# Stores of the gated scan output moved to GpSimd's queue, a third buffer for the chunk decays, and the group norm's roots turned on TensorE before they are written out

## The chip, the cores and the metric

One core of a Trainium2 chip runs the program. The core has TensorE (PE in the profile, with PEld for its weight loads), VectorE (DVE), ScalarE (ACT), GpSimd (POOL) and SyncE (SP), and 16 DMA engines that carry every transfer, whichever engine issued it. The metric is the device time of one execution in microseconds.

## The reference, cut to what matters

One sequence of 1024 rows of 1024 channels goes through a block of two mixers and an FFN, all in float32:

```
h  = rmsnorm(x);  u = h @ w_in              # split into z, xbc, dt, s_b, s_c, s_x, g_a, g_b
xbc = silu(causal_conv4(xbc) + b);  xs, B, C = split(xbc)
dt = softplus(dt_raw + dt_bias);  a = -exp(a_log)
y  = chunked_scan(xs, dt, a, B, C) + d_skip * xs       # 4 groups of 8 heads, head size 64, state 128
y  = y * silu(z)
y  = y * rsqrt(mean(y*y over the 512 channels of a group) + eps) * ssd_norm_w
branch_a = y @ w_ssd_proj
branch_b = (s_b * causal_conv3(s_c * s_x)) @ w_sconv_proj
x  = x + (sigmoid(g_a) * branch_a + sigmoid(g_b) * branch_b) @ w_o
x  = x + swiglu(rmsnorm(x));  out = rmsnorm(x)
```

The change touches the line with `rsqrt` (its root per row and group), the stores of the `y` that it makes, and the buffers of `exp(cumulated dt*a)` in the scan.

## The kernel before, in words

Every instruction is put on its engine in the order in which the Python code issues it; no scheduler moves anything. Semaphores are added where a tile, a buffer or a DRAM tensor is used again. An engine, and each engine's DMA queue, works strictly in that order: a DMA that waits holds up every later DMA of the same queue. A DMA issued from SP or ACT also waits until the eighth one before it, counted over both queues, has landed.

The large products are done with Strassen-Winograd forms (seven products of half-size blocks, named by `n` 1 to 7; T1 to T4 and S1 to S4 are sums of blocks). Every float32 operand is split into a high part (`hi`, by ACT) and a low part (`lo`, by DVE), and each product takes three matmuls (lines 81 to 83 and 673 to 675). SBUF is one pool of 47 pages of 4 KB a partition (`page`), given out in turn; what takes a page waits for the last user of it. PSUM is 8 banks (`bank`).

The program's stages on the profile's clock: the input product in half-size forms (up to about 620 us), the last 20 tiles of it computed directly (`direct_tile`, about 620 to 960 us), the products of the two mixers (`gv` and `gy`, tiles gb and gd), then `w_o`, and the FFN from about 1260 us on.

The scan runs inside the direct stage. `scans` is a generator; `direct_tile` advances it one step at a time between its matmuls, alternating `part1(j)` and `part2(j-1)` for the 32 pairs of group and 128-row chunk. `part1` reads the chunk (tiles bc, x1) and makes the masked decay matrix ab; `part2` makes poff (old state by C, multiplied by the decays eb), the new state st, and pdg. `part2(j)` ends with `prep_eb(j + 2)`: two DMAs of SP that fill an eb tile (line 387). The tag eb has two buffers, so that this DMA waits until DVE's line 476 of the same `part2(j)` has read the other use of the buffer.

After every fourth chunk `norm` starts, another generator that goes one piece forward in each scan step: it loads silu(z) (two DMAs of SP, line 507), multiplies (line 513), squares, sums over partitions with ones on TensorE (pq, line 527), makes the root (`rstd_of`, DVE and ACT, tiles gv and gr), writes the 128x4 roots to DRAM as 4 rows of 128 (line 530, GpSimd's queue) and reads them back broadcast over the partitions (rbc, line 532). Five steps later it scales y (line 537) and stores it to y_g from SP's queue (line 541). For the second half of a group it also makes T1 to T4 and stores them to yt_d (line 552). There are 8 norms: 8 root stores, 12 stores of y_g and 16 of yt_d. The last two norms end during the first product of the mixers, `gv`, where SP also loads its chunks (tiles ca and cb, from lines 728, 735 and 1098), four chunks ahead of TensorE; their high and low parts are made two chunks ahead.

Of the kernel before, what the change touches and what calls it, by code (L numbers as in the profile page):

```python
# [8 lines left out]
F32 = mybir.dt.float32  # L9
F32R = mybir.dt.float32r  # L10
AF = mybir.ActivationFunctionType
ALU = mybir.AluOpType

P = 128
S = 1024
D = 1024
KT = D // P
# [3 lines left out]
H = G * HPG  # L21
# [18 lines left out]
def hybrid_block(ctx: ExitStack, tc: tile.TileContext, x, nmw, w_in, cw, cb, dtb, alog, dsk, snw,  # L40
                 wssd, scw, wsc, wo, nfw, wg, wu, wd, fnw, out):
    nc = tc.nc
# [5 lines left out]
    cp = ctx.enter_context(tc.tile_pool(name="cp", bufs=1))  # L48
    pp = ctx.enter_context(tc.tile_pool(name="pp", bufs=NPAGES))
    sp = ctx.enter_context(tc.tile_pool(name="sp", bufs=2))  # L50
# [5 lines left out]
    def nm(s):  # L56
        cnt[0] += 1
        return f"{s}_{cnt[0]}"

    def page(s, shape=(P, 1024), dt=F32):  # L60
        return pp.tile(list(shape), dt, tag="pg", name=nm(s))

    def bank(s):
        return sm.tile([P, 512], F32, tag="sm", name=nm(s))
# [21 lines left out]
    ident = cp.tile([P, P], F32, name="ident")  # L86
# [9 lines left out]
    def rstd_of(ssq, n, s):  # L96
        shp = list(ssq.shape)
        v = sp.tile(shp, F32, tag="rv", name=nm(s + "v"))
        nc.vector.tensor_scalar(v, ssq, 1.0 / n, EPS, op0=ALU.mult, op1=ALU.add)
        r = sp.tile(shp, F32, tag="rr", name=nm(s + "r"))  # L100
        nc.scalar.activation(r, v, AF.Sqrt)
        nc.vector.reciprocal(r, r)
        q = sp.tile(shp, F32, tag="rq", name=nm(s + "q"))
        nc.vector.tensor_mul(q, r, r)
        nc.vector.tensor_mul(q, q, v)
        nc.vector.tensor_scalar(q, q, -0.5, 1.5, op0=ALU.mult, op1=ALU.add)
        nc.vector.tensor_mul(r, r, q)
        return r
# [20 lines left out]
    def rows_scale(src, xn, ssq, act=(), parts=1):  # L129
        r = rstd_of(ssq, D, "n")  # L130
        for c in range(parts):
            cs = slice(c * D // parts, (c + 1) * D // parts)
            for i in range(len(src)):
                if i in act:
                    nc.scalar.activation(xn[i][:, cs], src[i][:, cs], AF.Copy, scale=r[:, i:i + 1])
                else:
                    nc.vector.tensor_scalar_mul(xn[i][:, cs], src[i][:, cs], r[:, i:i + 1])
        return xn
# [85 lines left out]


    xt = [page("x") for _ in range(NT)]
    wdt_s = sp.tile([P, KT * H], F32, tag="eb", name="wdts").rearrange("p (k h) -> p k h", h=H)
    warm = cp.tile([P, 1], F32, name="warm")
    nc.scalar.activation(warm, epst, AF.Sqrt)
    for i in range(4):  # L230
        nc.sync.dma_start(xt[i], x[i * P:(i + 1) * P, :])


    ra = cp.tile([96, P], F32, name="ra")
    nc.gpsimd.dma_start(ra, cw[0].rearrange("k (i p) -> (k i) p", p=P))
    rb = cp.tile([80, P], F32, name="rb")
    nc.gpsimd.dma_start(rb[0:8, :], nmw.rearrange("o (i p) -> (o i) p", p=P))
    nc.gpsimd.dma_start(rb[8:16, :], nfw.rearrange("o (i p) -> (o i) p", p=P))
    nc.gpsimd.dma_start(rb[16:40, :], cb.rearrange("o (i p) -> (o i) p", p=P))
# [11 lines left out]
    def small_loads():  # L251
        nc.gpsimd.dma_start(d2, dsk.rearrange("o (i j) -> (o i) j", j=2))
        nc.gpsimd.dma_start(dtbc, dtb.rearrange("o h -> h o"))
        for q in range(4):
            nc.gpsimd.dma_start(al[32 * q:32 * q + 32, :], alog.rearrange("o h -> h o"))
    rd = cp.tile([16, 2, 64], F32, name="rd")
    cols = cp.tile([P, 192], F32, name="cols")
    cwc = lambda k, i: cols[:, k * 24 + i:k * 24 + i + 1]
    nmc = cols[:, 96:104]
# [14 lines left out]
    y_g = [dr.tile([512, S], F32, name=f"y_g{i}") for i in range(G)]  # L274
# [98 lines left out]
    bufs, cur = {}, {}  # L373
# [8 lines left out]
    def prep_eb(j):  # L382
        g, c = items[j]
        if c > 0:
            eb = bufs["e", j] = sp.tile([P, 4, P], F32, tag="eb", name=nm("eb"))
            for i in range(2):
                nc.sync.dma_start(eb[64 * i:64 * i + 64, :, :],
                                  e_d[c, g * HPG:g * HPG + HPG].rearrange("(r j) l -> j r l", j=2)[i].partition_broadcast(64))
# [70 lines left out]
    def part2(j):  # L459
# [37 lines left out]
        if c % 4 == 3:  # L497
            norms.append(norm(g, c // 4, *cur.pop(j // 4)["y"]))
        if j + 2 < len(items):
            prep_eb(j + 2)  # L500

    def norm(g, hf, y0, y1):

        ys, o = (y0, y1), slice(hf * 512, hf * 512 + 512)
        for i in range(2):
            z = page("z", HB)
            nc.sync.dma_start(z, z_g[g][256 * i:256 * i + 256, o].rearrange("(r p) l -> p r l", p=P))
            if i == 0:
                zs = z
        yield  # L510
        yield
        for y, z in zip(ys, (zs, z)):
            V.tensor_mul(y, y, z)
        yield
        yield
        sa, sb = page("sa", HB), page("sa", HB)
        nc.scalar.activation(sa, y0, AF.Square)
        nc.scalar.activation(sb, y1, AF.Square)
        yield
        V.tensor_add(sa, sa, sb)  # L520
        V.tensor_add(sa[:, 0], sa[:, 0], sa[:, 1])
        yield
        yield
        yield
        pq = bank("pq")
        for c in range(4):
            nc.tensor.matmul(pq[:, c:c + 1], sa[:, 0, c * P:(c + 1) * P], ones, start=True, stop=True)
        rs = rstd_of(pq[:, 0:4], INNER // G, "g")
        rd_ = rs_d[2 * g + hf]
        nc.gpsimd.dma_start(rd_.rearrange("c l -> l c"), rs)  # L530
        rbc = page("rbc", (P, 512))
        nc.gpsimd.dma_start(rbc, rd_.rearrange("c l -> (c l)").partition_broadcast(P))
        for _ in range(5):
            yield
        for r in range(4):
            z = ys[r // 2][:, r % 2]
            V.scalar_tensor_tensor(z, z, snc(4 * g + r), rbc, op0=ALU.mult, op1=ALU.mult)
            if r % 2:
                yield
                if hf == 0 or r > 1:  # L540
                    nc.sync.dma_start(y_g[g][128 * (r - 1):128 * (r + 1), o].rearrange("(r p) l -> p r l", p=P),
                                      ys[r // 2])
        if hf == 0:
            kept[g] = ys
            return

        b11, b21 = kept.pop(g)
        b12, b22 = ys
        t1, t2 = page("s1", HB), page("s2", HB)
        for t, a, b, f in ((t1, b11, b12, "T1"), (t2, t1, b22, "T2"), (b12, b12, b22, "T3"), (b21, b21, t2, "T4")):  # L550
            V.tensor_add(t, a, b)
            nc.sync.dma_start(yt_d[f][256 * g:256 * g + 256, :].rearrange("(k p) f -> p k f", p=P), t)
            yield

    def scans():


        def step_norms():
            for n in list(norms):
                if next(n, 0) == 0:  # L560
                    norms.remove(n)

        def one(f, j):
            f(j)
            step_norms()

        want(0, 0)
        want(0, 2)
        prep(0)
        prep(1)  # L570
        prep_eb(1)
        yield
        prep2(0)
        for j in range(len(items)):
            one(part1, j)
            yield
            if j > 0:
                one(part2, j - 1)
                yield
        one(part2, len(items) - 1)  # L580
        yield
        while norms:
            step_norms()
            yield
# [118 lines left out]
    def weight_forms(s, kind, kh):  # L703
        return {f"{kind}{i}": dr.tile([kh * P, 576], F32, name=f"{s}_d{i}")[:, 0:512] for i in range(1, 5)}
# [4 lines left out]
    vt_d, yt_d = weight_forms("vt", "T", 4), weight_forms("yt", "T", 8)  # L709
# [816 lines left out]
    nc.tensor.transpose(pc[:, 0:96], ra, ident[:96, :96])  # L1526
    nc.tensor.transpose(pc[:, 96:176], rb, ident[:80, :80])
    nc.scalar.activation(cols[:, 0:176], pc[:, 0:176], AF.Copy)
    r0 = rows_scale(*a0, act=(3,), parts=2)
    raw0, raw1 = ([], []), ([], [])  # L1530
    turned = {}
# [190 lines left out]
```

## Time and profile before

| | |
|---|---|
| median of 3 runs | 1922.33 us (1921.34 to 1922.79) |
| profiled execution | 1926.88 us, its span 1925.1 us, so 1.8 us lie around the span |
| TensorE busy | 1885.6 us, 98% of the span |
| DVE, ACT, GpSimd busy | 68%, 50%, 8% |
| granted clock of TensorE | 0.995 of full speed in the mean |
| DMA | 411.97 MB, 214 GB/s in the mean |
| DMA issues of SP's and ACT's queues | 323.27 and 29.36 MB; GpSimd's queue 57.79 MB |

TensorE is busy nearly all the time, so a change can gain only in the 39.5 us in which it is not, and in stretches in which its clock is granted at the lower of its two levels (1.2 in place of 2.4 GHz). The profiled execution is 0.24% longer than the median of the runs.

### The profile page before, as it was taken

The numbers are of one execution on the slowest core, as the hardware profiler recorded it, in microseconds if no ns is written. First come the engines' busy times: TensorE is split into PE (matmuls) and PEld (weight loads), VectorE is DVE, ScalarE is ACT, GpSimd is POOL, SyncE is SP. The second block draws the span as 40 slices with busy tenths as digits, with TensorE's granted clock in tenths as the row PEclk, the third lists the DMA queues.
The fourth block names the chain that finished last, engine by engine and source line by source line (L and its number), as shares of the span: only waits on it lengthen the run. The fifth ranks groups of instructions, "written<-read, shape, count | busy, mean of one in ns | idle before, by whom it ended". The sixth has DMA issues, their size and how long they took to land.

```text
span 1925.1 us, 24069 instructions
## 1 busy us (share of the span) xinstructions
PE 1885.6 (98%) x8897; PEld 1548.5 (80%) x8897; DVE 1299.5 (68%) x1688; ACT 969.8 (50%) x1533; POOL 151.0 (8%) x168
## 2 busy tenths in 40 slices
PE   7999999999999999999989999999999999999998
PEld 5688888888888888887768888887888888888886
DVE  7667878777775778897867648877444444456465
ACT  5545454445445987877655454464333333345333
POOL 1010111010100000000000000101221121100000
PEclk9999999999999999999989999999999999999999
DMA  5197999978959567888799866836998788867552
GB/s 179 58 258 176 241 230 236 230 203 224 276 137 292 184 210 212 263 239 227 210 265 328 292 220 211 202 122 141 222 207 210 195 193 200 218 259 286 195 194 111
DMA packets 344774, 411.97 MB, mean 214 GB/s; under 512 B 17416, under 2 KB 223936, under 8 KB 344656
## 3 DMA queue, kind: packets, MB, share of 16 engines
q1 hardware_dynamic: 292016, 323.27, 52.9%
q0 software_dynamic: 44576, 57.79, 18.8%
q10 hardware_dynamic: 8064, 29.36, 4.0%
q8 instruction: 70, 1.15, 0.2%
q14 instruction: 48, 0.39, 0.1%
HBM read 320.56 MB, written 143.15 MB: 241 GB/s over the span
## 4 chain that ended last, share of the span: by engine, by line
PE 84%; DMA 6%; DVE 5%; ACT 4%; issue 1%; SPq 0%; ACTq 0%; DVEq 0%
PE pb L673 5%; PE pb L674 5%; PE pb L675 5%; PE gb L673 5%; PE gb L674 5%; PE gb L675 5%; PE fb L675 4%; PE fb L674 4%; PE fb L673 4%; PE pd L673 4%; PE pd L674 4%; PE pd L675 4%; PE gd L675 3%; PE gd L673 3%; PE gd L674 3%; PE fd L675 3%
## 5 line engine op out<-in xcount | busy, mean ns | idle before, releaser
L77 DVE TENSOR_TENSOR wl<-ws,wh 128x1024 fp32r<-128x1024 f32 x77 | 94.0, 1222 | 121.2 <-ACT wh L76 121.2
L673 PE MATMUL gb<-qh,gh 128*128 128x512 f32 x432 | 168.9, 391 | 1.1 <-DVE h L1126 1.1
L674 PE MATMUL gb<-ql,gh 128*128 128x512 f32 x432 | 168.8, 391 | 0.0
L675 PE MATMUL gb<-qh,gl 128*128 128x512 f32 x432 | 168.8, 391 | 0.0
L675 PE MATMUL fb<-th,wl 128*128 128x512 f32 x352 | 137.0, 389 | 0.8 <-DVE wl L77 0.8
L673 PE MATMUL fb<-th,wh 128*128 128x512 f32 x352 | 137.1, 390 | 0.6 <-ACT wh L76 0.6
L674 PE MATMUL fb<-tl,wh 128*128 128x512 f32 x352 | 136.9, 389 | 0.0
L81 PE MATMUL pr<-th,wh 128*128 128x512 f32 x320 | 131.6, 411 | 0.0
L673 PE MATMUL gd<-qh,gh 128*128 128x512 f32 x324 | 127.2, 392 | 3.8 <-ACT qh L76 3.8
L83 PE MATMUL pr<-th,wl 128*128 128x512 f32 x320 | 125.7, 393 | 4.0 <-DVE wl L984 4.0
L674 PE MATMUL gd<-ql,gh 128*128 128x512 f32 x324 | 127.4, 393 | 0.8 <-DVE ql L77 0.8
L675 PE MATMUL gd<-qh,gl 128*128 128x512 f32 x324 | 127.2, 393 | 0.0
L82 PE MATMUL pr<-tl,wh 128*128 128x512 f32 x320 | 125.1, 391 | 0.0
L76 ACT ACTIVATE qh<-cb 128x1024 fp32r<-128x1024 f32 x98 | 99.9, 1020 | 40.1 <-PE gb L674 17.2
L77 DVE TENSOR_TENSOR ql<-cb,qh 128x1024 fp32r<-128x1024 f32 x98 | 116.0, 1184 | 3.9 <-ACT qh L76 3.7
L675 PE MATMUL fd<-th,wl 128*128 128x512 f32 x264 | 102.7, 389 | 0.0
L673 PE MATMUL fd<-th,wh 128*128 128x512 f32 x264 | 102.7, 389 | 0.0
L674 PE MATMUL fd<-tl,wh 128*128 128x512 f32 x264 | 102.7, 389 | 0.0
L74 DVE SCALAR_TENSOR_TENSOR gl<-ca,gh 128x1024 fp32r<-128x1024 f32 (+1 forms) x60 | 70.6, 1177 | 43.1 <-ACT gh L73 43.0
L673 PEld LDWEIGHTS gb<-qh,gh 128*128 128x128 f32 x432 | 81.5, 189 | 18.2 <-DVE h L1126 1.4
L674 PEld LDWEIGHTS gb<-ql,gh 128*128 128x128 f32 x432 | 81.4, 189 | 17.4 <-DVE ql L77 0.4
L673 PE MATMUL pb<-th,wh 128*128 128x512 f32 x240 | 94.5, 394 | 0.8 <-ACT u L888 0.8
(318 smaller groups left out, 4686.8 us busy)
## 6 DMA issues: line engine op xcount, KB each, us to landing
ws<-in_w_in_dram SPq DMA_DIRECT2D x80, 512.0 KB, 7.2
ws<-in_w_gate_dram SPq DMA_DIRECT2D x77, 256.0 KB, 3.9
ws<-in_w_up_dram SPq DMA_DIRECT2D x77, 256.0 KB, 4.5
ca<-u_d SPq DMA_DIRECT2D x35, 512.0 KB, 5.3
ab<-ac_d SPq DMA_DIRECT2D x32, 512.0 KB, 8.2
xbc_g<-cv ACTq DMA_DIRECT2D x24, 512.0 KB, 6.7
ws<-ws POOLq DMA_DIRECT2D x22, 512.0 KB, 6.4
wd_d<-in_w_down_dram SPq DMA_DIRECT2D x20, 512.0 KB, 9.5
```

The source lines that it names most:

```text
L74: nc.vector.scalar_tensor_tensor(lo, src, -1.0, hi.bitcast(F32), op0=ALU.mult, op1=ALU.subtract)
L76: nc.scalar.activation(hi, src, AF.Copy)
L77: nc.vector.tensor_sub(lo, src, hi.bitcast(F32))
L81: nc.tensor.matmul(o, lh, rh, start=first, stop=False)
L82: nc.tensor.matmul(o, lh, rl, start=False, stop=False)
L83: nc.tensor.matmul(o, ll, rh, start=False, stop=last)
L673: nc.tensor.matmul(o, lh, rh, start=first, stop=False, skip_group_check=True)
L674: nc.tensor.matmul(o, lh, rl, start=False, stop=False, skip_group_check=True)
L675: nc.tensor.matmul(o, ll, rh, start=False, stop=last, skip_group_check=True)
```

## The change: what it does

The 28 stores of y_g and yt_d are issued from GpSimd's queue, not from SP's. The tag eb gets a third buffer. For its room, the constants that are loaded at the start (ra and rb) stand in a page that is given back, and rd in a buffer of the tag st. In `norm`, two steps are put between the root and its store; in the second of them TensorE turns the 128x4 roots to 4x128 (prt), ACT copies them to SBUF (rst), and the store writes 4 whole rows. The wait that follows is four steps in place of five, so that the y of a norm is scaled and stored one step later.

```diff
-    wdt_s = sp.tile([P, KT * H], F32, tag="eb", name="wdts").rearrange("p (k h) -> p k h", h=H)
+    wdt_s = sp.tile([P, KT * H], F32, tag="eb", bufs=3, name="wdts").rearrange("p (k h) -> p k h", h=H)
...
-    ra = cp.tile([96, P], F32, name="ra")
+    consts = page("c")
+    ra, rb = consts[0:96, 0:P], consts[0:80, P:2 * P]
...
-    rd = cp.tile([16, 2, 64], F32, name="rd")
+    rd = sp.tile([P, 512], F32, tag="st", name="rd")[:16, 0:P].rearrange("a (b c) -> a b c", c=64)
...
-            eb = bufs["e", j] = sp.tile([P, 4, P], F32, tag="eb", name=nm("eb"))
+            eb = bufs["e", j] = sp.tile([P, 4, P], F32, tag="eb", bufs=3, name=nm("eb"))
...
         rs = rstd_of(pq[:, 0:4], INNER // G, "g")
+        yield
+        yield
+        prt = bank("prt")
+        nc.tensor.transpose(prt[:4, :P], rs, ident)
+        rst = sp.tile([4, P], F32, tag="rst", name=nm("rst"))
+        nc.scalar.activation(rst, prt[:4, :P], AF.Copy)
         rd_ = rs_d[2 * g + hf]
-        nc.gpsimd.dma_start(rd_.rearrange("c l -> l c"), rs)
+        nc.gpsimd.dma_start(rd_, rst)
         rbc = page("rbc", (P, 512))
         nc.gpsimd.dma_start(rbc, rd_.rearrange("c l -> (c l)").partition_broadcast(P))
-        for _ in range(5):
+        for _ in range(4):
             yield
...
-                    nc.sync.dma_start(y_g[g][128 * (r - 1):128 * (r + 1), o].rearrange("(r p) l -> p r l", p=P),
+                    nc.gpsimd.dma_start(y_g[g][128 * (r - 1):128 * (r + 1), o].rearrange("(r p) l -> p r l", p=P),
                                       ys[r // 2])
...
-            nc.sync.dma_start(yt_d[f][256 * g:256 * g + 256, :].rearrange("(k p) f -> p k f", p=P), t)
+            nc.gpsimd.dma_start(yt_d[f][256 * g:256 * g + 256, :].rearrange("(k p) f -> p k f", p=P), t)
```

On SP's queue, at the end of the direct stage, the loads of the first chunks of `gv` (ca, cb) and the last loads of eb and z stood between stores of y_g and yt_d; this is the order before:

```order
L387 DMA eb_7856<-e_d 64x4x128 x2
L728 DMA ca_7866<-in_w_sconv_proj_dram 128x2x512
L1098 DMA cb_7868<-v_g_128 128x2x512
L387 DMA eb_7964<-e_d 64x4x128 x2
L728 DMA ca_8014<-in_w_sconv_proj_dram 128x2x512
L1098 DMA cb_8016<-v_g_129 128x2x512
L541 DMA y_g_126<-y_6761 128x2x512
L552 DMA yt_d_163<-s_1223_8097 128x2x512
L507 DMA z_8101<-z_g_122 128x2x512
L507 DMA z_8103<-z_g_122 128x2x512
L552 DMA yt_d_164<-s_1224_8098 128x2x512
L728 DMA ca_8154<-in_w_sconv_proj_dram 128x2x512
```

And this is the same place of SP's queue in the changed program:

```order
L387 DMA eb_7872<-e_d 64x4x128 x2
L734 DMA ca_7889<-in_w_sconv_proj_dram 128x2x512
L1104 DMA cb_7891<-v_g_127 128x2x512
L387 DMA eb_7987<-e_d 64x4x128 x2
L734 DMA ca_8035<-in_w_sconv_proj_dram 128x2x512
L1104 DMA cb_8037<-v_g_128 128x2x512
L507 DMA z_8119<-z_g_121 128x2x512
L507 DMA z_8121<-z_g_121 128x2x512
L734 DMA ca_8172<-in_w_sconv_proj_dram 128x2x512
```

Loads alone are left there: the z loads and the third pair of ca and cb have no store ahead of them that waits for DVE.

On GpSimd's queue, in the direct stage, only the root stores (rs_d) and their broadcast loads (rbc) stood, as these rows before show:

```order
L697 DMA vt_d_162<-vt_d_160 256x512
L530 DMA rs_d_132<-gr_5524 128x4x1
L532 DMA rbc_5533<-rs_d_132 128x512
L530 DMA rs_d_133<-gr_5971 128x4x1
L532 DMA rbc_5980<-rs_d_133 128x512
```

In the changed program the same queue holds this, from the second norm on:

```order
L536 DMA rs_d_132<-rst_6092 4x128
L538 DMA rbc_6095<-rs_d_132 128x512
L547 DMA y_g_123<-y_5018 128x2x512
L558 DMA yt_d_162<-s_916_6399 128x2x512
L558 DMA yt_d_163<-s_917_6400 128x2x512
L558 DMA yt_d_164<-y_5017 128x2x512
L536 DMA rs_d_133<-rst_6525 4x128
L538 DMA rbc_6528<-rs_d_133 128x512
L558 DMA yt_d_165<-y_4654 128x2x512
L547 DMA y_g_124<-y_5432 128x2x512
```

The stores of one norm now stand around the root store of the next one; the store of T4 (yt_d_165) stands behind a broadcast load, which waits until its root store has landed.

On DVE, in `gv`, the low parts of the next chunk (gl, ql), the additions that empty the four gd banks (mc) and the scaling of y by rbc come ahead of the last norm's root (gv from pq); this is the order before:

```order
L537 SCALAR_TENSOR_TENSOR y_7198<-y_7198,cols,rbc_8138 128x512 x2
L77 TENSOR_TENSOR gl_8311<-ca_8212,gh_8310 128x1024
L77 TENSOR_TENSOR ql_8315<-cb_8214,qh_8314 128x1024
L1046 TENSOR_TENSOR mc_8248<-mc_8248,gd_8276 128x512
L1046 TENSOR_TENSOR mc_8248<-mc_8248,gd_8277 128x512
L1046 TENSOR_TENSOR mc_8249<-mc_8249,gd_8290 128x512
L1046 TENSOR_TENSOR mc_8249<-mc_8249,gd_8291 128x512
L537 SCALAR_TENSOR_TENSOR y_7199<-y_7199,cols,rbc_8138 128x512 x2
L99 TENSOR_SCALAR gv_8357<-pq_8352 128x4
```

In the changed program DVE has this there:

```order
L77 TENSOR_TENSOR gl_8336<-ca_8237,gh_8335 128x1024
L77 TENSOR_TENSOR ql_8340<-cb_8239,qh_8339 128x1024
L1052 TENSOR_TENSOR mc_8273<-mc_8273,gd_8303 128x512
L1052 TENSOR_TENSOR mc_8273<-mc_8273,gd_8304 128x512
L1052 TENSOR_TENSOR mc_8274<-mc_8274,gd_8317 128x512
L1052 TENSOR_TENSOR mc_8274<-mc_8274,gd_8318 128x512
L543 SCALAR_TENSOR_TENSOR y_7211<-y_7211,cols,rbc_8235 128x512 x2
L543 SCALAR_TENSOR_TENSOR y_7212<-y_7212,cols,rbc_8235 128x512 x2
L99 TENSOR_SCALAR gv_8383<-pq_8378 128x4
```

All four scalings by rbc have come to stand between the emptying of the banks and the last root. On TensorE that root is turned one chunk, 24 matmuls, after its sums; after the other seven sums there are two scan steps, or one chunk and the rest of a tile.

## Rows read from the trace of the kernel before

**Rows 1.** The page's first part: busy time, share of the span, instructions.

```profile
PE 1885.6 (98%) x8897; PEld 1548.5 (80%) x8897; DVE 1299.5 (68%) x1688; ACT 969.8 (50%) x1533; POOL 151.0 (8%) x168
```

**Rows 2.** Waits of PE, 600 to 1100 us: us in total, times, longest.

```profile
PE pr L83 <- DVE wl L984: 4.0, 1, 4.0
PE gd L673 <- ACT qh L76: 3.8, 1, 3.8
PE pq L527 <- DVE mc L1046: 2.6, 1, 2.6
PE poff L475 <- DVE st L484: 1.3, 1, 1.3
PE gd L674 <- DVE ql L77: 0.8, 1, 0.8
```

**Rows 3.** Stretches: PE, PEld, DVE, ACT, POOL busy, clock, DMA share, GB/s.

```profile
880.00:885.00 5.00, 5.00 (x26) 3.83 (x24) 1.11 (x1) 2.30 (x4) 0.00 (x0) 1.00 1.07 78
885.00:890.00 5.00, 1.05 (x3) 0.87 (x4) 3.47 (x4) 0.41 (x1) 0.54 (x1) 0.90 0.93 290
890.00:895.00 5.00, 5.00 (x33) 4.15 (x32) 4.66 (x9) 4.94 (x16) 0.00 (x0) 0.76 1.02 303
970.00:975.00 5.00, 5.00 (x23) 4.14 (x23) 1.83 (x2) 0.00 (x0) 0.00 (x0) 1.00 0.85 95
980.00:985.00 5.00, 3.67 (x9) 2.69 (x10) 2.36 (x3) 5.00 (x8) 0.00 (x0) 0.62 1.05 408
985.00:990.00 5.00, 5.00 (x17) 3.83 (x15) 4.97 (x7) 4.22 (x5) 0.00 (x0) 0.70 1.05 408
995.00:1000.00 5.00, 5.00 (x16) 3.93 (x16) 4.59 (x11) 4.47 (x6) 0.76 (x1) 0.67 0.70 211
```

**Rows 4.** Timeline, 868 to 890 us, of SP, POOL and DVE: start, length.

```profile
871.31 0.37 SPq L552 DMA_DIRECT2D yt_d<-s  x1
871.78 1.21 SPq L507 DMA_DIRECT2D z<-z_g  x2
...
873.44 0.77 POOL L530 DMA_DIRECT2D rs_d<-gr  x1 [26.05 <-DVE gr L107]
...
886.53 1.23 DVE L513 TENSOR_TENSOR y<-y,z 128x1024 f32<-128x1024 f32 x1 [5.42 <-DMA z<-z_g]
```

**Rows 5.** Timeline, 940 to 981 us, of SP and ACT.

```profile
954.33 0.36 SPq L541 DMA_DIRECT2D y_g<-y  x1
...
960.47 1.25 SPq L1098 DMA_DIRECT2D cb<-v_g  x1
...
979.46 1.06 ACT L76 ACTIVATE qh<-cb 128x1024 fp32r<-128x1024 f32 x1 [0.20 <-DMA cb<-v_g]
```

**Rows 6.** Waits of SP's queue, 600 to 1000 us: the longest in total, columns as in 2.

```profile
SPq L387 <- DVE st L484: 108.1, 14, 17.8
```

**Rows 7.** Line 430: TensorE turns a 128x128 tile once a scan pair.

```profile
L430 PE MATMUL pcb<-ident,bc x28: 272/273/273, 623.3 to 930.0; 128*128 128x128 f32 x28
```

**Rows 8.** DMA issues, 600 to 1000 us: count, KB each, median us to landing.

```profile
y_g<-y SPq DMA_DIRECT2D x11, 512.0 KB, 5.2
...
rbc<-rs_d POOLq DMA_DIRECT2D x7, 256.0 KB, 6.1
...
rs_d<-gr POOLq DMA_DIRECT2D x8, 2.0 KB, 12.5
```

**Rows 9.** Timeline of two norms: the sums on PE, the root's store on POOL.

```profile
827.09 1.05 PE L527 MATMUL pq<-ones,sa 128*128 128x1 f32 x8
...
832.74 0.76 POOL L530 DMA_DIRECT2D rs_d<-gr  x1 [28.30 <-DVE gr L107]
...
992.85 1.05 PE L527 MATMUL pq<-ones,sa 128*128 128x1 f32 x8 [2.62 <-DVE mc L1046]
...
997.53 0.76 POOL L530 DMA_DIRECT2D rs_d<-gr  x1 [19.82 <-DVE gr L107]
```

**Rows 10.** DVE's costliest line, 600 to 1000 us: busy us, mean ns, idle before.

```profile
L448 DVE TENSOR_TENSOR ab<-ab,cbm 128x1024 f32<-128x1024 f32 x32 | 39.0, 1219 | 0.4
```

More of the change, by code (lines that the diff above doesn't have):

```diff
@@ L231, in hybrid_block @@
         nc.sync.dma_start(xt[i], x[i * P:(i + 1) * P, :])
-    ra = cp.tile([96, P], F32, name="ra")
+    consts = page("c")
+    ra, rb = consts[0:96, 0:P], consts[0:80, P:2 * P]
     nc.gpsimd.dma_start(ra, cw[0].rearrange("k (i p) -> (k i) p", p=P))
-    rb = cp.tile([80, P], F32, name="rb")
     nc.gpsimd.dma_start(rb[0:8, :], nmw.rearrange("o (i p) -> (o i) p", p=P))
@@ L1528, in hybrid_block @@
     nc.scalar.activation(cols[:, 0:176], pc[:, 0:176], AF.Copy)
+    del consts, ra, rb
     r0 = rows_scale(*a0, act=(3,), parts=2)
```

## The prediction

> **What bounds the kernel now.** I read the page's first part first. The reader is to see that TensorE is busy for 1885.6 of 1925.1 us and that no other engine passes 68% [rows 1]. What can be gained is TensorE's idle time, and work that it does at the lower clock. So the second view is the list of TensorE's waits, in the part of the program that the change touches. It has five, 12.5 us together [rows 2], all between 884 and 993 us. The third view cuts that part into stretches of 5 us, for the granted clock. After three of the waits the clock is granted at the lower level. A mean clock of c over 5 us means that 10(1 - c) us of them ran at 1.2 GHz: 1.0 and 2.4 us after the first wait, 3.8 and 3.0 after the second, 3.3 after the wait of pq, 13.5 us in all [rows 3]. Half of that, 6.8 us, is lost. The stage therefore loses 12.5 + 6.8 = 19.3 us, and the start and the end of the program, where the other idle time lies, are not touched.
>
> Next, what was late. **The first wait** (pr, 4.0 us): DVE sat idle 5.4 us for the second z tile, and the low part wl that TensorE needed stood behind that multiplication. The z loads were issued from 871.8 us on, right behind a store of T2, and landed at 886.5, some 14 us later [rows 4]. **The second pair** (gd, 3.8 and 0.8 us): the high part qh waited for a load of cb, issued at 960.5 us and landed at 979.5 [rows 5]. In SP's order that load stands behind the y_g store, which SP issued only at 954.3, once DVE had scaled y.
>
> Two causes stand behind each. SP's queue waits: before eb loads alone it stood 108 us for DVE [rows 6], and before the stores as well, with all loads behind it. And the transfers stall: 7 us after the root store at 873.4 [rows 4] the 16 engines move 78 GB/s, and again 95 GB/s at 970 to 975, though their share of busy time stays at 1.07 and 0.85 [rows 3]; the mean is 214. That store has 512 elements of 4 bytes, and its 2 KB take 12.5 us to land, where 512 KB of y take 5.2 [rows 8]. Packets that hold the engines without moving bytes, a few us behind such a store, are what I take for its effect.
>
> **The change part by part.**
>
> Stores to GpSimd's queue, third eb buffer: no work is added or taken away. The eb load now waits for a reader one scan pair back, 10.2 us earlier (30 pairs between 623.3 and 930.0 us [rows 7]), and the ca, cb and z loads have no store ahead of them. Loads then go out as soon as their page is free. What a page waits for next is a matmul or DVE's work several steps back, so I expect lead times of 5 to 10 us more. GpSimd issues 28 DMAs more; at 0.8 us each [rows 4] that is 22 us on an engine that is 8% busy [rows 1], and nothing on another engine waits for it closely. A y_g or T tile is read by `gy` only, four or more chunks later.
>
> Here a rule speaks against the change. DVE is busy through the stretch, its costliest line a two-input operation of 1219 ns for 1024 elements [rows 10], and GpSimd's issues beside it take 0.76 to 0.77 us each time [rows 4, 9]. The Trainium skill (SBUF — State Buffer, section "SBUF: two separate sides") says that descriptors of GpSimd's DMAs are written through a port that DVE can lock in its fast modes, and that such DMAs then stall. By it the 28 stores would land late; by the rows they would not, and no run here shows such a stall.
>
> Roots turned: 8 transposes, by the nearest row 0.27 us each [rows 7], 2.2 us on TensorE. From below they cost nothing (where TensorE would idle anyway); from above, no more than the group of column sums pq, 1.05 us [rows 9], so 8.4. I take 2.2, because that row also turns one tile with the same identity between products. ACT's copies of 4x128 lie beside ACT's idle half [rows 1].
>
> Root stores: 4 rows of 512 bytes in place of 512 elements. Bounds for the landing: 12.5 us as now, or about the 5.2 to 6.1 of large transfers [rows 8]. I take the lower, and the stall as gone.
>
> The added steps: a root is ready, with its store issued, 5.7 us after the sums in the loop and 4.7 in the last norm [rows 9]. In the loop the turn comes two steps of 5.1 us later [rows 7], so it has 4.5 us to spare. In the last norm it comes one chunk later: 24 matmuls at 23 in 5 us [rows 3] are 5.2 us, with pq itself 6.3. DVE has two more scalings of 512 columns ahead of that root, some 1.2 us by half of 1.22 each [rows 10]; 4.7 + 1.2 = 5.9. That is close. Also close there is rbc: four chunks, 20.8 us, for turn, copy and two issues (about 2 us), the landing and 6.1 us of broadcast: 20.6 us with today's landing, 13 with an ordinary one.
>
> **The sum.** Removed: the first wait and its clock, 4.0 + 1.7; poff, 1.3, where DVE was behind for the same late loads; the second pair and its clock, 3.8 + 0.8 + 3.4. That is 15.0. The wait of pq and its clock, 2.6 + 1.7, I leave in: pq waits until DVE has emptied a bank, and if that goes, the last turn or rbc stands close enough to take its place. Added: 2.2. Net -12.8 us. The profiled execution of 1926.9 us would become 1914.1. It is 4.6 us longer than the median of the runs, and how much of that lies in these waits is not shown; I take the sum off the median: 1922.3 - 12.8 = **1909.5 us**.
>
> Bounds: with pq's wait gone as well and turns for nothing, -19.3, 1903.0. With turns at 8.4, -6.6, 1915.7.
>
> **The rivals.** *Pages wait behind GpSimd's queue.* T4's store stands behind a broadcast load, which waits for the root store to land; a load that takes T4's page then waits in SP's queue, and all loads behind it. Landing 5 to 12 us plus the store's own 5.2 [rows 8] puts that page 10 to 17 us behind the turn, about two or three steps. It would bring back one of the two large waits, 5.7 to 8.0 us: 1922.3 - 12.8 + 6.9 = about 1916. For it: 47 pages in turn, and three such places. Against: loads are issued two steps or more ahead.
>
> *The loads come no earlier where it counts.* If the engines' bandwidth is what is short, or the stall has another cause than 4-byte elements, both waits stay, and the turns are paid: 1922.3 + 2.2 = 1924.5, at most 0.1% off. For it: 408 GB/s at 980 to 990 us [rows 3], so that the engines do fill up. The Trainium skill (DMA: Bandwidth & Descriptors, section "Issuing engines are not separate DMA queues") says that all queues share the same 16 engines and that another queue saves only the time of issuing. By that rule the move of the stores would gain 28 short issues, and nothing on the path. Against: SP's 108 us of standing are order, not bandwidth [rows 6], and before both waits the engines moved less than half of the mean [rows 3].
>
> *TensorE waits for the turned roots* (the other side). Should DVE be later than 10.2 us with a root, TensorE, which works in order, stands at the transpose, and the clock falls behind it: the like of pq's wait, 2.6 + 1.7 = 4.3 us each. Three such waits eat the 12.8; from four on the change is slower: 1909.5 + 17.2 = about 1927, and 1944 with all eight. Against: 4.5 us to spare in the loop [rows 7, 9], and DVE gets its inputs earlier.
>
> **How the numbers follow.** Forecast 0.66, pages 0.14, no change 0.11, turned roots 0.09. About 0.2%, 3.8 us, is what a measurement of this kernel tells from no change. The first two are faster, 0.80; then 0.11 and 0.09. The range reaches from 1903 to 1920: above it lie the last two cases alone, and the likeliest case's own range is 1903 to 1916.
>
> **What would show it.** In the trace after: no wait of pr for wl and of gd for qh near 885 and 975 us, SP's queue without waits for DVE at eb, no 5 us stretch under 100 GB/s behind a root store, roots landing in about 5 us, a clock of 1.00 from 885 to 1000 us, and 8 transposes of about 0.27 us. I am wrong if TensorE's waits come back at prt, or at pr or pst behind ACT and DVE that wait for loads; or if the waits go and others of the same size appear later in `gv`, where SP now fills the pages earlier.

## The result, and the profile after

The changed kernel takes 1909.3 us in the median (1908.28 to 1910.68, 6 runs), the kernel before 1922.56 us beside it (1918.72 to 1924.15, 6 runs). The ratio is 0.9934, with an interval of 0.9922 to 0.9947: 13.3 us less. The profiled execution took 1910.68 us, against 1926.88 before.

The page's first part of the changed kernel, as in [rows 1]:

```profile
PE 1879.7 (98%) x8905; PEld 1545.3 (81%) x8905; DVE 1299.4 (68%) x1688; ACT 970.6 (51%) x1541; POOL 169.7 (9%) x196
```

TensorE's waits between 600 and 1100 us, as in [rows 2]; a wait is named by the tile that TensorE is about to write. One is left of five, and it is a new one, the wait for a turned root:

```profile
PE prt L532 <- DVE gr L107: 2.1, 1, 2.1
```

Stretches of 5 us, columns as in [rows 3]:

```profile
880.00:885.00 5.00, 5.00 (x27) 4.19 (x26) 4.04 (x5) 2.20 (x6) 1.25 (x2) 1.00 0.97 352
885.00:890.00 5.00, 5.00 (x38) 4.00 (x37) 5.00 (x9) 4.94 (x15) 1.29 (x2) 1.00 0.98 284
...
970.00:975.00 5.00, 5.00 (x26) 4.00 (x24) 5.00 (x7) 4.62 (x5) 1.28 (x2) 1.00 0.97 336
...
980.00:985.00 5.00, 2.88 (x12) 2.03 (x12) 4.59 (x11) 3.04 (x5) 1.93 (x3) 0.92 0.63 184
985.00:990.00 5.00, 5.00 (x18) 3.95 (x18) 4.98 (x5) 2.78 (x5) 0.04 (x1) 0.74 0.98 333
```

At 880 to 885 us the engines move 352 GB/s where they moved 78, and at 970 to 975 us 336 in place of 95, at about the same share of busy time. The clock is full up to 980 us. What is lost in the stage is now 2.1 us of waiting and, at the lower clock, (0.08 + 0.26) x 5 = 1.7 us; before it was 12.5 + 6.8.

DMA issues between 600 and 1000 us, as in [rows 8]:

```profile
y_g<-y POOLq DMA_DIRECT2D x11, 512.0 KB, 6.0
...
yt_d<-y POOLq DMA_DIRECT2D x6, 512.0 KB, 7.4
...
rbc<-rs_d POOLq DMA_DIRECT2D x8, 256.0 KB, 5.3
...
rs_d<-rst POOLq DMA_DIRECT2D x8, 2.0 KB, 5.7
```

The root's 2 KB land in 5.7 us where they took 12.5. Waits of SP's queue between 600 and 1000 us, as in [rows 6]:

```profile
SPq L387 <- DVE st L484: 24.0, 9, 14.4
...
SPq L387 <- DVE xx L476: 12.3, 4, 6.2
...
SPq L369 <- DMA yt_d<-y: 10.3, 2, 7.3
```

At eb SP stands 24 us for DVE's st where it stood 108. The last row is the start of the rival of the pages: SP waits for pages that a store on GpSimd's queue still reads. With the loads of lines 1104, 741 and 735 it stands 27.2 us for such stores. No wait of TensorE follows from it.

The seventh and the eighth norm, from the timeline of POOL, DVE and PE:

```profile
965.03 0.53 POOL L536 DMA_DIRECT2D rs_d<-rst  x1
972.20 0.57 POOL L538 DMA_DIRECT2D rbc<-rs_d  x1 [6.64 <-PE gd L681]
...
979.12 2.74 DVE L543 SCALAR_TENSOR_TENSOR y<-y,cols,rbc 128x512 f32<-128x512 f32 x4 [2.89 <-DMA rbc<-rs_d]
...
983.22 0.27 PE L532 MATMUL prt<-ident,gr 128*4 128x128 f32 x1 [2.12 <-DVE gr L107]
```

This is where the wait left over comes from. The seventh root is turned at 958.0 us, but its store goes out only at 965.0, behind the stores that now share GpSimd's queue. Its broadcast goes out 6.6 us after that. The view puts this wait down to a product (gd), but the store itself landed 6.6 us after 965.0, and the broadcast goes out 0.6 us after the landing; in e7, e9 and e11 below the same store lands after 7.1, 6.7 and 11.4 us, and the broadcast follows it by 0.5 to 0.6 us each time. So it is the landing that the broadcast waits for. DVE stands 2.9 us for it ahead of four scalings, and the eighth root, behind these in DVE's order, is late for its turn.

### The profile page after: what moved, and what is told of

The parts are those of the page before. It is cut to its first block, busy times and chain, and to the rows that moved or that the text cites. A ratio compares the mean times of both kernels' runs of the same rounds, so it can differ in the third digit from the quotient of the medians.

```text
span 1908.9 us, 24143 instructions
## 1 busy us (share of the span) xinstructions
PE 1879.7 (98%) x8905; PEld 1545.3 (81%) x8905; DVE 1299.4 (68%) x1688; ACT 970.6 (51%) x1541; POOL 169.7 (9%) x196
## 4 chain that ended last, share of the span: by engine, by line
PE 92%; DVE 4%; ACT 2%; DMA 1%; issue 1%; SPq 0%; ACTq 0%; DVEq 0%
PE pb L679 5%; PE pb L680 5%; PE pb L681 5%; PE gb L679 5%; PE gb L680 5%; PE gb L681 5%; PE fb L681 4%; PE fb L679 4%; PE fb L680 4%; PE pr L81 4%; PE pr L83 4%; PE pr L82 4%; PE gd L679 4%; PE pd L679 4%; PE gd L681 4%; PE gd L680 4%
## 5 line engine op out<-in xcount | busy, mean ns | idle before, releaser
L681 PEld LDWEIGHTS gb<-qh,gl 128*128 128x128 f32 x432 | 81.5, 189 | 17.1
```

The source lines that it names most:

```text
L681: nc.tensor.matmul(o, ll, rh, start=False, stop=last, skip_group_check=True)
```

## The experiments

Twelve kernels, each timed in up to five rounds beside the kernel before, whose median was 1923.3 to 1923.7 us in these comparisons. "Waits" are TensorE's between 600 and 1100 us in the profiled execution, "clock" is the sum of (1 - c) x 5 us over the 5 us stretches of 700 to 1015 us. Every kernel of the table but that of before has the edits that make room at the start (ra, rb and rd), and those with three eb buffers also that of wdts; the cuts of the diffs leave these lines out.

| run | stores on | eb buffers | steps | root store | median us | ratio to before | waits + clock us | profiled us |
|---|---|---|---|---|---|---|---|---|
| before | SP | 2 | old | 512 x 4 B | 1922.6 | | 12.5 + 6.8 | 1926.9 |
| full change | GpSimd | 3 | new | 4 rows | 1909.3 | 0.9934 [0.9922, 0.9947] | 2.1 + 1.7 | 1910.7 |
| e1_queue | GpSimd | 2 | old | 512 x 4 B | 1912.2 | 0.9943 [0.9931, 0.9955] | 4.4 + 1.7 | 1913.4 |
| e2_eb3 | SP | 3 | old | 512 x 4 B | 1919.6 | 0.9986 [0.9977, 0.9995] | 10.2 + 6.8 | 1924.1 |
| e3_queue_eb3 | GpSimd | 3 | old | 512 x 4 B | 1914.2 | 0.9958 [0.9946, 0.9970] | 3.9 + 3.5 | 1914.2 |
| e4_roots | SP | 2 | new | 4 rows | 1909.2 | 0.9926 [0.9913, 0.9938] | 1.5 + 1.7 | 1910.3 |
| e5_steps | SP | 2 | new | 512 x 4 B | 1914.8 | 0.9955 [0.9943, 0.9968] | 4.5 + 1.7 | 1913.6 |
| e6_roots_small | SP | 2 | new | 4 rows, and 512 x 4 B unread | 1912.9 | 0.9949 [0.9937, 0.9962] | 4.3 + 0 | 1911.9 |
| e7_full_small | GpSimd | 3 | new | 4 rows, and 512 x 4 B unread | 1909.5 | 0.9927 [0.9913, 0.9940] | 1.0 + 0 | 1909.8 |
| e8_roots_queue | GpSimd | 2 | new | 4 rows | 1910.5 | 0.9931 [0.9919, 0.9944] | 1.6 + 0 | 1908.3 |
| e9_full_late | GpSimd | 3 | new, last turn later | 4 rows | 1907.2 | 0.9917 [0.9903, 0.9930] | 0 + 0 | 1907.4 |
| e10_rq_late | GpSimd | 2 | new, last turn later | 4 rows | 1907.1 | 0.9917 [0.9903, 0.9930] | 0 + 0 | 1906.6 |
| e11_full_4byte | GpSimd | 3 | new | 512 x 4 B | 1914.4 | 0.9956 [0.9943, 0.9968] | 5.4 + 3.4 | 1914.3 |
| e12_roots_eb3 | SP | 3 | new | 4 rows | 1909.1 | 0.9933 [0.9919, 0.9946] | 0.8 + 0 | 1908.6 |

One sum holds for all of them: the profiled time is 1907.4 us, that of e9 which has no loss, plus waits plus clock. It gives 1926.7 for before, 1911.2 for the full change, 1913.5 for e1, 1924.4 for e2; it is off by at most 1.4 us, and by 1.9 in e11.

### Which part carries it: one part alone

**e1_queue.** The stores alone:

```diff
-                    nc.sync.dma_start(y_g[g]...
+                    nc.gpsimd.dma_start(y_g[g]...
...
-            nc.sync.dma_start(yt_d[f]...
+            nc.gpsimd.dma_start(yt_d[f]...
```

> The stores of y_g and yt_d on GpSimd's queue alone: two eb buffers, 4-byte root stores and the steps as before. Order, by the stores: the waits of SP for DVE at the two stores (about 50 us) go, the z and cb loads go out earlier, and the waits of pr and gd with their clock (15.0 us) go: about 1907 to 1911 us. Order, by eb: SP still stands over 100 us for DVE at eb, both waits stay: about 1920 to 1923. Stalls: the 8 root stores still land in 10 us or more, stretches under 100 GB/s follow them, both waits stay: about 1922. The pages rival (T4's store behind a broadcast load that waits some 12 us) would show here at its worst: 1922 or more.

1912.2 us, just above the range of the order by the stores and far from the other three. TensorE's waits:

```profile
PE pq L527 <- DVE mc L1046: 2.6, 1, 2.6
PE pr L83 <- DVE wl L984: 1.8, 2, 0.9
```

The wait of gd is gone, that of pr is down from 4.0 to 1.8 us, that of pq is as before. SP still stands 138.9 us for DVE's st at eb, so it was the stores and not eb that held the loads up.

**e2_eb3.** The third buffer alone:

```diff
-            eb = bufs["e", j] = sp.tile([P, 4, P], F32, tag="eb", name=nm("eb"))
+            eb = bufs["e", j] = sp.tile([P, 4, P], F32, tag="eb", bufs=3, name=nm("eb"))
```

> The third eb buffer alone (with the edits that make its room): stores on SP, 4-byte root stores, steps as before. Order, by eb: SP's 108 us of standing for DVE at eb fall below 40, both large waits go: 1907 to 1912 us. Order, by the stores: SP now stands at the stores instead, both waits stay: 1920 to 1923. Stalls: no change, 1922.

1919.6 us, a gain of 0.1% with an interval that nearly reaches 0. The waits:

```profile
PE pq L527 <- DVE mc L1046: 4.1, 1, 4.1
PE pr L83 <- DVE wl L984: 3.0, 1, 3.0
PE gd L673 <- ACT qh L76: 2.3, 1, 2.3
PE gd L674 <- DVE ql L77: 0.8, 1, 0.8
```

SP's standing for st at eb falls from 108.1 to 17.0 us, and the waits of pq, pr and gd are still there; SP stands at the y_g stores instead, 55.8 us. This profiled execution, 1924.1 us, is among the slowest of the kernel's twelve (1917.7 to 1924.1), so that a usual one loses less.

**e3_queue_eb3.** Both, roots as before:

> Both order edits, roots untouched: 4-byte stores, five steps as before. Order theory: TensorE's waits of 15.0 us go and the 2.2 us of turns are not paid: 1905 to 1909 us, faster than the full change. Stalls theory: the root stores still hold the engines for 5 to 10 us, one or both of the waits of pr and gd stay (4 to 8 us each with the clock), 1914 to 1922. Both needed: in between, and slower than the full change at 1909.3.

1914.2 us: the two don't add, and the third buffer gains nothing on top of e1. The waits, and DVE at the last norm:

```profile
PE pq L527 <- DVE mc L1046: 3.2, 1, 3.2
PE pr L83 <- DVE wl L984: 0.7, 1, 0.7
```

```profile
974.49 1.41 DVE L537 SCALAR_TENSOR_TENSOR y<-y,cols,rbc 128x512 f32<-128x512 f32 x2 [2.93 <-DMA rbc<-rs_d]
...
978.09 2.47 DVE L1046 TENSOR_TENSOR mc<-mc,gd 128x512 f32<-128x512 f32 x4
```

But for 0.7 us of pr the loads are early now, and what is left is the root's landing, 13.4 us for the seventh: DVE stands 2.9 us for rbc with the emptying of the banks (mc) behind it, and pq waits for a bank.

**e4_roots.** The turned roots with their steps alone, stores on SP, two eb buffers:

> The turned roots alone, with their added steps: stores on SP, two eb buffers. Stalls theory: no stretch under 100 GB/s behind a root store, loads land in 5 to 8 us, the waits of pr and gd go: 1908 to 1913 us. Order theory: SP still stands over 100 us for DVE at eb, both waits stay and the turns are paid: 1922 to 1926. Root landing 5 to 7 us by both.

1909.2 us, all of the gain. SP's queue and the place of the stall, with TensorE's one wait:

```profile
PE pq L527 <- DVE mc L1052: 1.5, 1, 1.5
```

```profile
SPq L387 <- DVE st L484: 105.5, 17, 18.0
```

```profile
880.00:885.00 5.00, 5.00 (x27) 4.15 (x27) 4.04 (x5) 2.20 (x6) 0.51 (x1) 1.00 1.07 387
```

SP stands at eb as long as before, and neither pr nor gd waits for a load. One load is still late: ACT stands 3.8 us for a ca (line 741) that SP issued at 964.4 us, right behind a store of yt_d that had waited for DVE, and the emptying of the banks, with pq's 1.5 us, follows from it. At the same share of busy time as before, 1.07, the engines move 387 GB/s in place of 78. This kernel has the added steps as well as the turn; the next one parts the two.

### Shape of the store, or its place

**e5_steps.** The kernel before with the steps of the change, without the turn:

```diff
         rs = rstd_of(pq[:, 0:4], INNER // G, "g")
+        yield
+        yield
         rd_ = rs_d[2 * g + hf]
         nc.gpsimd.dma_start(rd_.rearrange("c l -> l c"), rs)
...
-        for _ in range(5):
+        for _ in range(4):
```

> The kernel of before with the two added steps and the four steps of waiting, and nothing else: the root store still writes 512 elements of 4 bytes, some 10 us later in the program than before. If it is the shape of the store that counts (stalls), the root stores land in 11 us or more, stretches under 100 GB/s stay, the waits of pr and gd return in part, moved by 10 us: 1914 to 1923 us. If it is the later place of the root store and of the scaling of y alone, the turn was not needed: 1905 to 1910 us.

1914.8 us: between the two, 8.9 us less than the kernel before of its comparison (1923.66) and 5.6 more than e4. In this kernel the root store is still issued right behind the root (at 872.4 us, 873.4 before, for one norm; at 953.6, 960.5 before, for the seventh), because GpSimd doesn't wait for TensorE's steps; what the steps move is the scaling of y, with the stores and sums behind it. The later root store that I had named was no part of this edit.

```profile
PE pq L527 <- DVE mc L1048: 4.0, 1, 4.0
PE poff L475 <- DVE st L484: 0.5, 1, 0.5
```

```profile
880.00:885.00 5.00, 5.00 (x27) 4.19 (x26) 4.05 (x5) 2.07 (x5) 0.00 (x0) 1.00 1.00 112
```

The stall is there again (112 GB/s), but the z loads stand behind one store of yt_d less and just make it: issued 0.5 us earlier than before, they land in 7.4 us at most, not 14.2, and pr doesn't wait. The cb load whose chunk was late goes out 7.4 us earlier (953.1 us, 960.5 before) and lands in 6.3 us in place of 19.0. The time is in the range of the stalls theory, but not by its mechanism: neither pr nor gd waits. The steps gain without the turn, and what the turn adds lies elsewhere: the ca behind SP's store of yt_d lands in 9.7 us here and in 7.3 in e4, and the wait of pq that follows is 4.0 and 1.5 us.

**e6_roots_small.** e4 with the old root store added, to a tensor that nobody reads:

```diff
+    rx_d = [dr.tile([4, P], F32, name=f"rx_d{i}") for i in range(2 * G)]
...
+        nc.gpsimd.dma_start(rx_d[2 * g + hf].rearrange("c l -> l c"), rs)
```

> The turned roots alone, as in e4_roots, and on top of it, at the old place right behind the root, a store of the same 512 elements of 4 bytes to a DRAM tensor that nobody reads. Stalls theory: stretches under 100 GB/s come back a few us behind each of these 8 stores, other loads land late, and the time returns to 1915 to 1923 us although nothing waits for the stores themselves. Landing theory (what counted was only that rbc waited 12 us for the root): the time stays at 1908 to 1911 us.

1912.9 us, 3.8 more than e4: more than the landing theory allowed, less than the theory of the stalls asked for.

```profile
PE pq L528 <- DVE mc L1054: 1.9, 1, 1.9
PE prt L534 <- DVE gr L107: 1.5, 1, 1.5
PE poff L476 <- DVE st L485: 0.9, 1, 0.9
```

```profile
960.00:965.00 5.00, 5.00 (x23) 4.13 (x22) 5.00 (x6) 3.38 (x6) 0.38 (x1) 1.00 1.18 86
```

Nothing waits for the added stores, and at 960 us the engines move 86 GB/s at a share of 1.18 (e4: 203 at 0.57). The true roots land in 8.3 us in place of 5.1, so the two theories are not quite parted here.

**e7_full_small.** The same stores added to the full change:

> The full change with the same 8 unread stores of 512 elements of 4 bytes added on GpSimd's queue. Stalls theory: the stalls are back, but SP's loads go out earlier, so less of them reaches TensorE: 1912 to 1917 us, near the 1914.2 of both order edits without the roots. If they cost nothing: 1909.

1909.5 us: they cost nothing, as the second case had it. The stall is there, 45 GB/s at a share of 0.80 where the full change moved 352 at 0.97, and TensorE's one wait is that of prt:

```profile
PE prt L534 <- DVE gr L107: 1.0, 1, 1.0
```

```profile
880.00:885.00 5.00, 5.00 (x27) 4.19 (x26) 4.04 (x5) 2.20 (x6) 1.25 (x2) 1.00 0.80 45
```

**e11_full_4byte.** The full change with its steps, root stored as before:

```diff
-        prt = bank("prt")
-        nc.tensor.transpose(prt[:4, :P], rs, ident)
...
-        nc.gpsimd.dma_start(rd_, rst)
+        nc.gpsimd.dma_start(rd_.rearrange("c l -> l c"), rs)
```

> The full change with its steps, but the root stored as before, 512 elements of 4 bytes, without turn and copy. If the turn is needed in the full change (landing of 12 us and the stalls): 1912 to 1916 us, as both order edits without steps gave 1914.2. If stores, eb and steps leave room enough, the turn is worth nothing here: 1907 to 1910 us, the less by up to 2.2 us of transposes.

1914.4 us, 5.1 more than the full change. Beside e7, where the stalls were back at no cost, this points to the landing. The 4-byte stores of e7 stand in other places (952.5 us at the seventh norm, 965.2 here), so the two runs alone don't part landing and stall; the times of this run do.

```profile
PE gd L676 <- DVE ql L77: 3.0, 1, 3.0
PE gd L675 <- ACT qh L76: 2.4, 1, 2.4
```

GpSimd's queue, DVE and ACT in the timeline of this run:

```profile
977.19 0.55 POOL L534 DMA_DIRECT2D rbc<-rs_d  x1 [11.25 <-DMA cb<-vt_d]
...
984.05 2.74 DVE L539 SCALAR_TENSOR_TENSOR y<-y,cols,rbc 128x512 f32<-128x512 f32 x4 [7.68 <-DMA rbc<-rs_d]
...
986.89 0.21 ACT L101 ACTIVATE gr<-gv 128x4 f32<-128x4 f32 x1 [12.20 <-DVE gv L99]
```

The chain: the seventh root's store goes out at 965.2 us as in the full change (965.0), lands after 11.4 us in place of 6.6, and the broadcast follows at 977.2 in place of 972.2, 5.0 us later, which is what the run lost. So rbc is late, DVE stands 7.7 us for it, the small step of the last root (gv) is behind the scalings, ACT's square root stands 12.2 us for gv, and behind it in ACT's order stand the high parts for which TensorE waits.

### The rest of the table, and a better version

**e8_roots_queue** and **e12_roots_eb3** leave one part out of the full change, the third buffer or the move of the stores:

> The full change without the third eb buffer: turned roots and the stores on GpSimd's queue, two eb buffers. If the third buffer is worth nothing once the stalls are gone: 1907 to 1910 us. If it costs 2 us, as e3 against e1 suggests (1914.2 against 1912.2): 1907. If it carries part of the gain: 1911 or more, with SP standing over 100 us for DVE at eb again.

> The full change with the stores left on SP's queue: turned roots with their steps and three eb buffers. If the moved stores are worth nothing once the roots are turned, as e4_roots suggests: 1907 to 1911 us. If SP, freed from eb, stands at the stores instead and that costs: 1912 us or more, with a wait of pr or gd.

1910.5 us, between the ranges of e8's cases, and 1909.1, in that of e12's first. Beside the full change's runs (1908.3 to 1910.7) neither part is worth a measurable amount next to the turned roots. In e8 SP stands longer at eb than in the kernel before, and TensorE's one wait is that of prt, 1.6 us:

```profile
SPq L387 <- DVE st L484: 122.5, 17, 17.8
```

**e9_full_late** and **e10_rq_late** turn the last root one chunk later, with and without the third buffer:

```diff
-        yield
-        yield
+        for _ in range(3 if (g, hf) == (3, 1) else 2):
+            yield
         prt = bank("prt")
...
-        for _ in range(4):
+        for _ in range(3 if (g, hf) == (3, 1) else 4):
             yield
```

> The full change with the turn of the last norm one chunk of gv later, and one step less of waiting behind it, so that the scaling of y stays where it is. The wait of TensorE for that root (2.1 us in the profile of the full change) and the half clock behind it (0.08 x 5 + 0.26 x 5 = 1.7 us) go: 1909.3 - 3.8 = about 1905.5 us. If rbc is then late for the scaling: the wait moves to DVE and from there to the emptying of banks, 1908 to 1911.

> The same later turn without the third eb buffer (e8_roots_queue with it). There the wait for the root was 1.6 us: 1907 us if the wait and its clock go, 1910 if not. Beside e9_full_late it says again whether the third buffer is worth anything: less than 1 us between them if not.

1907.2 and 1907.1 us, 2.1 us under the full change and the fastest of all. The runs of the full change (1908.3 to 1910.7) all lie above theirs (1906.6 to 1907.6), though the three were not timed in the same rounds and the intervals of their ratios overlap. TensorE has no wait between 600 and 1100 us in either. In e9's timeline the turn finds its root ready, and its clock stays full:

```profile
986.49 0.27 PE L532 MATMUL prt<-ident,gr 128*4 128x128 f32 x1
```

```profile
980.00:985.00 5.00, 5.00 (x24) 4.14 (x23) 4.59 (x11) 3.69 (x5) 1.43 (x2) 1.00 0.64 182
```

I had expected 1905.5, because I took 3.8 us of one profiled execution off the median. Off the profiled time it is 1910.7 - 3.8 = 1906.9, and e9's was 1907.4.

## Why the prediction was right, step by step

**The terms removed** (15.0 us) went: no wait of pr, poff or gd is left, and the clock is full up to 980 us.

**The wait of pq, left in at 4.3 us,** went too, and the wait for the last turned root took its place, 2.1 + 1.7 = 3.8 us, as the step had allowed. That e9 removes it by moving this one turn shows that it was the wait for the root.

**The turns were mis-sized,** 2.2 us forecast. Each has the 0.27 us of the nearest row, but not on the path. The timeline of PE around one of them in the changed kernel:

```profile
957.77 0.39 PE L681 MATMUL gb<-qh,gl 128*128 128x512 f32 x1
958.00 0.27 PE L532 MATMUL prt<-ident,gr 128*4 128x128 f32 x1
958.03 0.48 PE L679 MATMUL gb<-qh,gh 128*128 128x512 f32 x1
958.34 0.40 PE L680 MATMUL gb<-ql,gh 128*128 128x512 f32 x1
```

The third product matmul of one group and the second of the next start 0.57 us apart where two steps of 0.23 would be 0.46: some 0.1 us for a turn, 0.9 for eight. The sum over all runs, which needs no term for the turns, agrees to within what it is off by, 1.4 us (1.9 in e11). A matmul's duration in the profile overlaps its neighbours'; its price is the distance of starts.

**The total** matched by two errors that cancel, and that they cancel is luck. In the profiled executions the stage gave 16.2 us (1926.9 to 1910.7), more than 12.8: all of 19.3 - 3.8 = 15.5, and the turns cost nearly nothing. But that execution of before lay 4.3 us above the median of its runs, and part of its waits with it. The prediction had said that this was not shown; the eight runs of e9 and e10, whose profiled executions have no waits in this stage, lie within 1.0 us, those of before between 1918.7 and 1925.9, which suggests that the scatter is in the waits.

**The causes** were half right. "Two causes stand behind each" names SP's order and the stalls. That the stores in SP's order were a cause e1 shows: taking them away removes the wait of gd and over half of that of pr. That the stalls were needed as well for these two waits no run shows. e4, which is without the stalls, has the added steps too, and e5, which has the steps and keeps both causes, has no wait of pr or gd either: its loads go out before the stall. Taking stores and stalls away together gains nothing over e4 (the full change). For gd the prediction names a load of cb alone; ACT had stood much longer for the ca of the same chunk, issued at 960.0 us and landed 18.2 us later, as this row of the kernel before shows:

```profile
978.20 1.06 ACT L76 ACTIVATE gh<-ca 128x1024 fp32r<-128x1024 f32 x1 [12.73 <-DMA ca<-in_w_sconv_proj_dram]
```

The step that failed is the weight of eb. I read SP's 108 us of standing there as what delays the loads; e2 removes most of it and keeps the waits, e4 and e8 keep it and have no wait of pr or gd. The DMAs behind eb were early enough to stand.

**The stall** behind a store of 4-byte elements is shown by e6 and e7, where such a store is added and nothing reads it. Between 700 and 1015 us every kernel with such a store has 5 us stretches under 115 GB/s at a share of 0.6 or more; the six without one have none at a share above 0.44. What it costs depends on the slack: 3.8 us with SP's old order, part of it through the roots behind it that land later, and nothing with the new. **The landing** of the root, which I had treated as harmless beside it, is the dearer half once the loads are early: 5.1 us in e11 against the full change.

**The test that I named was too blunt.** After the change there still are 5 us stretches under 100 GB/s, such as 87 GB/s at 925 to 930 us, but at a share of 0.30: engines without work. A stall is a low rate at a high share. Of the other signs, the waits of pr and gd, the landing and the transposes came out as named; SP still stood 36 us for DVE at eb (24.0 and 12.3), the clock fell to 0.92 and 0.74 at 980 to 990 us, and the one wait at prt, which I had named as a sign of being wrong, cost 3.8 us.

**The rivals.** Pages behind GpSimd's queue: SP waits for them (27.2 us) and TensorE doesn't. No gain: ruled out by e1 alone, where the move of 28 stores gained 11.2 us, by the order in which loads wait behind stores. The Trainium skill (DMA: Bandwidth & Descriptors, section "Issuing engines are not separate DMA queues") holds that another issuing engine saves only the time of issuing; e1 disagrees wherever a store that waits has loads behind it. TensorE waiting for a turned root: once of eight, at the last, where 4.7 + 1.2 us had to fit into 5.2 to 6.3; it took 8.7 us from the sums (974.5) to the turn (983.2), DVE's 2.9 us for rbc among them. Beside DVE at work, GpSimd's stores of y were issued in 0.71 to 0.75 us each, and y_g landed in 6.0 us (5.2 from SP). The rule of the Trainium skill that the prediction weighed there (SBUF — State Buffer, section "SBUF: two separate sides"), by which DVE can hold up the descriptors of GpSimd's DMAs, shows nowhere in these rows. Whether DVE ran in one of its fast modes beside them no row tells, so they don't decide on the rule.

What stays open: why pr's wait shrank but did not go in e1, what the turn gives without the added steps, which was not run, and whether the turn's step could be saved by a place for the seventh root's store ahead of the T stores in GpSimd's queue, which was not tried.

## What to carry to other kernels

A stall for a late load has several sufficient cures: look for the cheapest one, and try each part alone before stacking them, because here one of three parts, the turned roots with their steps, gave everything (14.3 us, 8.9 of them by the steps alone) and the other two nothing on top. Store a few scalars a partition as whole rows, turned on TensorE between other products: 2 KB written as 512 elements land 7 us later and slow the transfers behind them. A queue's long standing is no evidence by itself; ask whether what stands behind it is late for its reader.

## What the runs showed of the hardware that was not expected

A store of 512 elements of 4 bytes takes 11.2 to 12.5 us to land in the median, in every kernel that has it, and each of these kernels has stretches of 5 us that move as little as 21 to 112 GB/s at shares of 0.6 to 1.3, where 300 to 400 GB/s at a share of 1 are usual. The same 2 KB as four rows land in 4.3 to 6.2 us, but in 8.3 to 8.6 when such a store stands ahead of it. A transpose of 128x4 put between two products costs TensorE 0.1 us, less than half of its 0.27 us in the profile.
